# A decoder trunk on one core: sixteen tiles of the first FFN by seven block products, with sums of weights made by DMA

## The chip, the cores and the metric

The kernel runs on one core of a Trainium2 chip. The core has TensorE (matmuls, with a separate path for loading the stationary operand), VectorE, ScalarE and GpSimd for element-wise work, and DMA queues issued from SyncE (SP), ScalarE and GpSimd. In the profile they are PE (PEld for its weight loads), DVE, ACT, POOL and SP. The metric is the device time of one execution in microseconds; a kernel is given by the median of its runs.

## The reference

The reference is a trunk of two layers on a residual stream x of 512 tokens by 1024 channels, in float32. Layer 0 is a Conformer convolution module, layer 1 a RetNet retention; each is followed by a ConvFFN, and a last RMSNorm ends it. Each block reads `rmsnorm(x, g)`, that is x times rstd (one number per token) times a gain per channel, and is added to x. The change is in the FFN of layer 0:

```python
def conv_ffn(x, w_in, dw_w, dw_b, w_out):
    h = x @ w_in                              # (512, 1024) @ (1024, 2 * 2816)
    a, u = jnp.split(h, 2, axis=-1)
    a = causal_dwconv(a, dw_w, dw_b)          # width 3 over the tokens
    return (jax.nn.silu(a) * u) @ w_out       # (512, 2816) @ (2816, 1024)
```

## The kernel before

**Layout.** The residual lies in SBUF transposed: eight tiles `xT[k]` of 128 channels by 512 tokens. The 2816 inner channels of an FFN are 22 inner tiles of 128 channels. A result tile of the first matmul is 128 inner channels by 512 tokens, one PSUM bank; there are eight banks.

**Three products for one.** Every float32 operand is split into a high part, rounded to TensorE's fast float32 format (`fp32r`), and a low part, the rest; a product is three matmuls, high by high, low by high and high by low (`mm3`, lines 271 to 274). ScalarE makes the high part of weights (line 229), VectorE the low part (line 233), in pieces of 128 x 1024; four buffers of each part are there (`wh`, `wl`), and four for raw weights (`wr`), which SP loads from DRAM (line 202). The function `weights()` (line 265) hands out the next unit of weights and emits the loading and splitting of the unit after it. Units are used in the order in which `_chunks()` (line 75) lists them.

**The FFN.** `HALVES` (line 29) cuts the 22 inner tiles into groups of 12 and 10. For each group `ffn_half` (line 785) makes, per inner tile, eight `mm3` for a and eight for u on the split x times gain, 48 matmuls of 512 columns. The factor rstd is applied afterwards, as it is only known by then: `evac` (line 804) multiplies a by the broadcast rstd `norm.rb` (line 812, VectorE), applies the three taps (line 814 on ScalarE, lines 815 and 816 on VectorE) and Silu (line 817), multiplies by rstd once more for u (line 818, GpSimd), then by u (line 820, VectorE), and splits the result y. `evac` of a tile is emitted after the matmuls of the next one. `proj_out` (line 398) then multiplies the y of a group by `w_out` and adds to `xT` (line 430, VectorE); with a `norm` given, it also begins the next normalisation. Its weights come in chunks of up to four inner tiles.

**What else runs there.** The rotary tables of layer 1 (`rotary_tables`, line 836) are a generator of GpSimd steps; in the first FFN one step is issued per inner tile, tied behind that tile's scaling and product by `issue_after` (line 823).

**Seven products in layer 1.** `ret_vg_blocks` (line 1013) makes the v and gate of a retention head by a Strassen-Winograd scheme on two-by-two blocks: seven block products in place of eight. The sums on the side of x are made once, by `left_sums` (line 916) from x times gain times rstd (`normed`, line 911); sums of weights are made on VectorE in SBUF (line 255). Its matmuls have 512 columns.

**Order.** Each engine has one queue that it works off in order. A planner lays out the instructions from the traced program; `issue_after` and `pe_in_order` tie an instruction behind another one of the same engine.

## Time and profile before

| | before |
|---|---|
| median of 3 runs | 1293.9 us (1293.53 to 1294.2) |
| the profiled execution | 1293.24 us, span 1291.5 us |
| first FFN in the trace | 182.3 to 543.5 us |
| TensorE, VectorE, ScalarE, GpSimd busy | 1282.0, 810.0, 520.9, 355.2 us |
| TensorE's granted clock | 0.999 |
| moved by DMA | 140.48 MB, mean 109 GB/s |

The span runs from the first to the last instruction of the profiled execution; some 1.7 us of its time lie around it. A row of instruction groups gives line, engine, operation, output and inputs, shape, count, then busy time, mean duration in ns, and idle time before it with what ended that. A row of the windows gives, per engine, busy time and the number of instructions. A matmul's duration includes its way through the array, so matmuls overlap, and their pace is the distance between two starts.

### The profile page before, as it was taken

What the parts mean: (1) busy time and instruction counts of PE and PEld (TensorE: products, weight loads), DVE (VectorE), ACT (ScalarE), POOL (GpSimd) and SP (SyncE); (2) the same over time, 40 slices, a digit from 0 to 9 for tenths busy, and PEclk for the clock granted to TensorE, in tenths of its full rate; (3) what the DMA queues carried; (4) which work ended last, traced back from release to release, by engine and by line L of the source; (5) the groups of instructions that cost most, each with busy time, mean ns of one, the idle gap of its engine ahead of it and who ended that gap; (6) DMA issues with size and microseconds to landing.
All of it is one profiled execution on the core that took longest, in us unless ns stands there. A gap on an engine that the chain in (4) does not pass through costs nothing.

```text
span 1291.5 us, 15110 instructions
## 1 busy us (share of the span) xinstructions
PE 1282.0 (99%) x5955; PEld 1067.0 (83%) x5955; DVE 810.0 (63%) x1036; ACT 520.9 (40%) x703; POOL 355.2 (28%) x305
## 2 busy tenths in 40 slices
PE   9999999999999999999999999999999999999997
PEld 7889988888888888888888888878888888888886
DVE  6998657665335554579696596596675643355542
ACT  6646644333124333334435335354443431233332
POOL 0957323797006110221311312304211110011111
PEclk9999999999999999999999999999999999999999
DMA  9533422313221313323314405323224342213111
GB/s 330 225 123 106 148 98 70 127 66 130 98 98 66 130 49 114 131 81 106 106 42 160 138 14 180 103 83 116 97 76 145 94 143 98 98 66 131 33 65 65
DMA packets 35926, 140.48 MB, mean 109 GB/s; under 512 B 10896, under 2 KB 15760, under 8 KB 21776
## 3 DMA queue, kind: packets, MB, share of 16 engines
q1 hardware_dynamic: 32256, 134.02, 30.2%
q10 hardware_dynamic: 3600, 5.52, 1.5%
q8 instruction: 46, 0.75, 0.2%
q14 instruction: 24, 0.20, 0.0%
HBM read 130.08 MB, written 2.10 MB: 102 GB/s over the span
## 4 chain that ended last, share of the span: by engine, by line
PE 96%; DVE 2%; issue 1%; ACT 0%; POOL 0%; POOLq 0%
PE fa L272 6%; PE fa L274 6%; PE fu L273 6%; PE fu L272 6%; PE fu L274 6%; PE fa L273 6%; PE lo L272 3%; PE fo L273 3%; PE fo L274 3%; PE lo L273 3%; PE lo L274 3%; PE fo L272 3%; PE cph L539 2%; PE ro L272 2%; PE ro L273 2%; PE ro L274 2%
## 5 line engine op out<-in xcount | busy, mean ns | idle before, releaser
L233 DVE TENSOR_TENSOR wl<-wr,wh 128x1024 fp32r<-128x1024 f32 (+2 forms) x242 | 302.7, 1254 | 207.2 <-ACT wh L229 203.7
L229 ACT CAST wh<-wr 128x1024 fp32r<-128x1024 f32 (+2 forms) x244 | 250.5, 1029 | 372.0 <-PE fo L274 82.7
L811 POOL MEMSET ap<- 128x2 f32 x44 | 4.2, 99 | 371.7 <-DVE ft L816 305.4
L988 POOL TENSOR_TENSOR gg<-gg,gn 128x512 f32<-128x512 f32 x16 | 27.5, 1719 | 179.3 <-ACT gg L987 179.3
L820 DVE TENSOR_TENSOR fy<-fu,ft 128x512 f32<-128x512 f32 x44 | 30.4, 690 | 68.6 <-PE fu L274 35.0
L814 ACT ACTIVATE ft<-ap,prm 128x512 f32<-128x512 f32 x44 | 35.8, 814 | 71.3 <-DVE ap L812 71.3
L588 DVE SCALAR_TENSOR_TENSOR tp<-hp,prm,tp 128x512 f32<-128x512 f32 x80 | 55.8, 747 | 0.4
L579 POOL TENSOR_TENSOR pla<-pla,plt 128x512 f32<-128x512 f32 x36 | 49.1, 1365 | 9.8 <-ACT pla L575 5.7
L815 DVE SCALAR_TENSOR_TENSOR ft<-ap,prm,ft 128x512 f32<-128x512 f32 x44 | 37.2, 844 | 17.7 <-ACT ft L814 17.5
L817 ACT ACTIVATE ft<-ft 128x512 f32<-128x512 f32 x44 | 27.9, 633 | 45.0 <-DVE ft L816 44.6
L972 POOL TENSOR_TENSOR rs<-rs 128x512 f32<-128x512 f32 x16 | 24.7, 1559 | 67.5 <-DVE rs L971 43.7
L818 POOL TENSOR_TENSOR ft<-ft,n3r 128x512 f32<-128x512 f32 x22 | 32.1, 1461 | 29.0 <-ACT ft L817 29.0
L818 POOL TENSOR_TENSOR ft<-ft,n1r 128x512 f32<-128x512 f32 x22 | 31.6, 1434 | 28.8 <-ACT ft L817 28.8
L816 DVE SCALAR_TENSOR_TENSOR ft<-ap,prm,ft 128x512 f32<-128x512 f32 x44 | 35.8, 814 | 1.5
L578 ACT ACTIVATE plt<-hp,prm 128x512 f32<-128x512 f32 x36 | 25.8, 722 | 20.6 <-POOL pla L579 20.2
L539 PEld LDWEIGHTS cph<-ph,cmat 128*128 128x128 f32 x288 | 32.6, 192 | 0.2
L539 PE MATMUL cph<-ph,cmat 128*128 128x128 f32 x288 | 32.6, 275 | 0.0
L430 DVE TENSOR_TENSOR xT<-ro,xT 128x512 f32<-128x512 f32 x32 | 21.6, 682 | 15.6 <-PE ro L274 15.6
L255 DVE TENSOR_TENSOR wr<-wr,wr 128x1024 f32<-128x1024 f32 x24 | 28.8, 1211 | 0.0
L812 DVE TENSOR_TENSOR ap<-fa,n3r 128x512 f32<-128x512 f32 x22 | 15.1, 690 | 20.5 <-PE fa L274 20.5
L812 DVE TENSOR_TENSOR ap<-fa,n1r 128x512 f32<-128x512 f32 x22 | 15.1, 689 | 17.2 <-PE fa L274 17.2
L856 POOL TENSOR_SCALAR near<-prod 128x512 f32<-128x512 f32 x11 | 22.9, 2085 | 0.9
(1851 smaller groups left out, 3842.1 us busy)
## 6 DMA issues: line engine op xcount, KB each, us to landing
wr<-in_weights_dram SPq DMA_DIRECT2D x106, 1024.0 KB, 4.9
cmat<-in_mats_dram SPq DMA_DIRECT2D x4, 2304.0 KB, 10.6
wr<-in_weights_dram SPq DMA_DIRECT2D x4, 512.0 KB, 3.4
wr<-in_weights_dram SPq DMA_DIRECT2D x6, 256.0 KB, 6.8
yt<-yq ACTq DMA_DIRECT2D x24, 64.0 KB, 2.1
yt<-yq SPq DMA_DIRECT2D x24, 64.0 KB, 2.1
xt<-xq SPq DMA_DIRECT2D x32, 48.0 KB, 2.0
xT<-in_xt_dram SPq DMA_DIRECT2D x4, 256.0 KB, 4.4
```

Source lines behind the costliest of these rows:

```text
L229: latest[0] = act.copy(hi[:, o:o + n], raw[:, s + o:s + o + n])
L233: latest[1] = low_on.get(i, dve).tensor_tensor(out=lo[:, o:o + n], in0=raw[:, s + o:s + o + n], in1=hi[:, o:o + n].bitcast(F32), op=ALU.su ...
L272: pe.matmul(ps, wh, xh, start=first, stop=False, **check)
L273: pe.matmul(ps, wl, xh, start=False, stop=False, **check)
L274: pe.matmul(ps, wh, xl, start=False, stop=last, **check)
L539: pe.matmul(ps[:, g * P:(g + 1) * P], mats[i][g][:, s, :], ph[:, g, NSH - 1 - s:NSH - 1 - s + P], start=s == 0, stop=s == NSH - 1)
L579: gate[0] = pool.tensor_tensor(out=pl, in0=pl, in1=tm, op=ALU.add).ins
L588: dve.scalar_tensor_tensor(out=a, in0=hp[:, t:t + S], scalar=tap(t, i), in1=a, op0=ALU.mult, op1=ALU.add)
L814: act.activation(t, ap[:, 2:], AF.Identity, scale=wc(2), bias=wc(3))
L815: dve.scalar_tensor_tensor(out=t, in0=ap[:, 1:1 + S], scalar=wc(1), in1=t, op0=ALU.mult, op1=ALU.add)
L816: dve.scalar_tensor_tensor(out=t, in0=ap[:, 0:S], scalar=wc(0), in1=t, op0=ALU.mult, op1=ALU.add)
L818: scaled = pool.tensor_tensor(out=t, in0=t, in1=norm.rb, op=ALU.mult)
```

## The change

- The first FFN has four groups of inner tiles, 6, 6, 6 and 4 (`GROUPS[0]`). The first stays as it was, the other sixteen tiles go by `ffn_blocks`. The second FFN keeps 12 and 10.
- `ffn_blocks` takes two inner tiles at a time: four weight blocks (two halves of the 1024 input channels, times the a and u parts, 256 columns each) against four blocks of x (two halves of the channels, two halves of the tokens). Seven products each go over 2 tiles x 4 blocks of 128 channels x 3 matmuls of 256 columns (256 tokens). They accumulate into banks z, x and p, six of the eight; between products ScalarE copies z out (`kept`, q1, u1, u2), and VectorE forms the four results from banks and copies.
- x is taken times gain and rstd (`Factors`), so that these tiles need no rstd afterwards: the pass of line 818 and that of line 812 fall away for them. The sums on the side of x (`sums_of`) are made on VectorE and ScalarE during the first group, and all eight x tiles are multiplied and split anew (`normed_split`) into the slots of the old ones behind it.
- The four sums of weights, a, b, c and d, are made in DRAM per group (`make_sums`): eight DMAs issued from GpSimd, in the order of its instructions, four of them copies and four adding to what is there. Each is 128 x 1024 float32 per pair of tiles, for a whole group at once. Those of the second group are issued during the first, those of each later group during the one before. The loads of the products then take single blocks or sums of 512 KB, seven to a pair.
- The rotary steps all go beside the first group, two to a tile, without the tie behind the tile's own work.

```diff
-HALVES = [(0, 12), (12, 22)]
+GROUPS = [[(0, 6, False), (6, 12, True), (12, 18, True), (18, 22, True)], [(0, 12, False), (12, 22, False)]]
...
-        for f0, f1 in HALVES:
-            for f in range(f0, f1, 2):
+        for f0, f1, by_blocks in GROUPS[l]:
+            if by_blocks:
+                pairs.append((len(out), (f1 - f0) // 2))
+                for kc, part in ((0, 0), (0, 1), (1, 0), (1, 1)):
+                    for f in range(f0, f1, 2):
+                        cols("ffn_w_in", l, 512 * kc, 4, (F * part + f * P, 256))
+            for f in range(f0, f1, 2) if not by_blocks else ():
...
+    def pool_in_order():
+        return tc.issue_after(next(i for i in reversed(nc.cur_bb.bb.instructions) if i.engine == mybir.EngineType.Pool))
...
+        n = dict(pairs).get(i)
+        if n:
+            units += [(i, (j, which)) for j in range(n) for which in (0, 2, "a", "b", "c", "d", 3)]
+            i += 4 * n
+            continue
...
+        if isinstance(n, tuple):
+            j, which = n
+            raw = wp.tile([P, 2048], F32, tag="wr", bufs=4, name=f"wr{i}_{j}{which}")
+            src = block(i, which)[:, j] if isinstance(which, int) else made[i][which][:, j]
+            nc.sync.dma_start(raw[:, :1024], src)
+            for _ in split_raw(raw, i, unit):
+                pass
+            return
...
+    def make_sums(i):
+        made[i] = {which: dp.tile([P, dict(pairs)[i], 1024], F32, tag="sum", bufs=8, name=f"sum{i}{which}")
+                   for which in "abcd"}
+        a, b, c, d = (made[i][which] for which in "abcd")
+        def copy(dst, src):
+            with pool_in_order():
+                pool.dma_start(dst, src)
+        def add(dst, src):
+            with pool_in_order():
+                pool.dma_start(dst, src, accum_op=ALU.add)
+        copy(a, block(i, 0))
+        copy(c, block(i, 1))
+        yield
+        add(a, block(i, 1))
+        add(c, block(i, 3))
+        yield
+        copy(b, a)
+        yield
+        add(b, block(i, 3))
+        yield
+        copy(d, b)
+        yield
+        add(d, block(i, 2))
...
+    class Factors:
+        def __init__(self, norm, xs, pool_, other):
+            self.norm, self.xs, self.other = norm, xs, other
+            self.sums = [pool_.tile([P, 4, 4, N2], F32R, tag=f"s{half}", bufs=1, name=f"{norm.name}s{half}") for half in "hl"]
+        def normed(self, k):
+            n = self.norm
+            t = xp.tile([P, S], F32, tag="nsq", bufs=2, name=f"{n.name}n{k}")
+            dve.scalar_tensor_tensor(out=t, in0=xT[k], scalar=n.gain[:, k:k + 1], in1=n.rb, op0=ALU.mult, op1=ALU.mult)
+            return t
+        def sums_of(self, k):
+            x1, x2 = self.normed(k), self.normed(k + 4)
+            lo, hi = slice(0, N2), slice(N2, S)
+            a = xp.tile([P, 2, N2], F32, tag="nacc", bufs=1, name=f"{self.norm.name}sa{k}")
+            b = self.other(f"{self.norm.name}sb{k}")
+            dve.tensor_tensor(out=a[:, 0], in0=x1[:, hi], in1=x2[:, hi], op=ALU.subtract)
+            dve.tensor_tensor(out=a[:, 1], in0=a[:, 0], in1=x1[:, lo], op=ALU.subtract)
+            dve.tensor_tensor(out=b[:, 0], in0=x1[:, lo], in1=x1[:, hi], op=ALU.subtract)
+            dve.tensor_tensor(out=b[:, 1], in0=x2[:, lo], in1=a[:, 1], op=ALU.add)
+            for o, t in ((0, a), (2, b)):
+                h, l = (u[:, k, o:o + 2, :] for u in self.sums)
+                act.copy(h, t)
+                dve.tensor_tensor(out=l, in0=t, in1=h.bitcast(F32), op=ALU.subtract)
+        def normed_split(self, k):
+            self.xs[k] = split(self.normed(k), f"{self.norm.name}n{k}", ("xh", "xl"), xp8)
...
+    def ffn_blocks(fp, l, norm, f0, f1, left, side=None):
+        ys = []
+        for f in range(f0, f1, 2):
+            def bank(which):
+                return [psum(f"f{which}{l}_{f + j}")[:, :N2] for j in range(2)]
+            def product(pss, which, first=False):
+                w = weights()
+                for j, ps in enumerate(pss):
+                    for k, (xh, xl) in enumerate(left.factor(which)):
+                        mm3(ps, *w(k, j * P, (j + 1) * P), xh, xl, first and k == 0, k == 3, skip_group_check=not first)
+            def kept(pss, name):
+                tiles = [fp.tile([P, N2], F32, tag=name, bufs=2, name=f"{name}{l}_{f + j}") for j in range(2)]
+                for t, ps in zip(tiles, pss):
+                    act.copy(t, ps)
+                return tiles
+            lo, hi = slice(0, N2), slice(N2, S)
+            aps = [fp.tile([P, S + 32], F32, tag="ap", bufs=2, name=f"ap{l}_{f + j}") for j in range(2)]
+            us = [fp.tile([P, S], F32, tag="fy", bufs=2, name=f"fy{l}_{f + j}") for j in range(2)]
+            z = bank("z")
+            product(z, "x11", True)
+            q1 = kept(z, "q1")
+            x = bank("x")
+            product(x, "x12", True)
+            for j in range(2):
+                dve.memset(aps[j][:, :2], 0.0)
+                dve.tensor_tensor(out=aps[j][:, 2:2 + N2], in0=x[j], in1=q1[j], op=ALU.add)
+            p = bank("p")
+            product(p, "s1", True)
+            product(z, "s2")
+            u1 = kept(z, "u1")
+            product(z, "s3")
+            u2 = kept(z, "u2")
+            for j in range(2):
+                dve.tensor_tensor(out=us[j][:, hi], in0=p[j], in1=u2[j], op=ALU.subtract)
+            product(z, "x22")
+            ts = []
+            for j in range(2):
+                act.copy(aps[j][:, 2 + N2:2 + S], z[j])
+                ts.append(taps(fp, l, f + j, aps[j]))
+            product(p, "s4")
+            for j in range(2):
+                dve.tensor_tensor(out=us[j][:, lo], in0=p[j], in1=u1[j], op=ALU.subtract)
+                dve.tensor_tensor(out=us[j], in0=us[j], in1=ts[j], op=ALU.mult)
+                ys.append(split(us[j], f"y{l}_{f + j}", ("yh", "yl"), fp))
+            if side is not None:
+                next(side, None)
+                next(side, None)
+        return ys
...
+            t = taps(fp, l, f, ap)
...
+            if each is not None:
+                next(each, None)
...
-        fp = es.enter_context(tc.tile_pool(name="f0", reuse_waits="tile", bufs=12))
+        fp = es.enter_context(tc.tile_pool(name="f0", reuse_waits="tile", bufs=6))
         rp = es.enter_context(tc.tile_pool(name="rot", reuse_waits="tile", bufs=1))
-        n2 = Norm(mix_g[1], "n2")
+        groups = GROUPS[0]
+        making = [make_sums(i) for i, _ in pairs[:len(groups) - 1]]
         rot = rotary_tables(rp)
-        for n, (f0, f1) in enumerate(HALVES):
-            ys = ffn_half(fp, 0, n1, f0, f1, () if n else (None, n1.stats, n1.bcast), rot)
-            proj_out(ys, f"fo{n}", n2 if n else None)
+        left = Factors(n1, list(n1.xs), fp, lambda name: fp.tile([P, 2, N2], F32, tag="fy", bufs=2, name=name))
+        def each():
+            for f in range(groups[0][1] - 1):
+                next(making[0], None)
+                next(rot, None)
+                next(rot, None)
+                if f:
+                    left.sums_of(f - 1)
+                yield
+        next(making[0])
+        ys = ffn_half(fp, 0, n1, *groups[0][:2], (None, n1.stats, n1.bcast), each=each())
         for _ in rot:
             pass
+        for k in range(KD):
+            left.normed_split(k)
+        for _ in making[0]:
+            pass
+        proj_out(ys, "fo0", None)
+        for n, (f0, f1, _) in enumerate(groups[1:], 1):
+            side = making[n] if n < len(making) else None
+            ys = ffn_blocks(fp, 0, n1, f0, f1, left, side)
+            for _ in side or ():
+                pass
+            n2 = Norm(mix_g[1], "n2") if n == len(groups) - 1 else None
+            proj_out(ys, f"fo{n}", n2)
...
```

More of the change, by code (lines that the diff above doesn't have):

```diff
@@ L75, in _chunks @@
 def _chunks():
-    out, blocks = [], []
+    out, blocks, pairs = [], [], []
     def cols(w, l, r0, nk, *ranges):
@@ L128, in _chunks @@
     ffn(1)
-    return out, blocks
+    return out, blocks, pairs
 LINE = 256
@@ L258, in emit_weights, with block @@
             pass
+    made = {}
+    def block(i, which):
+        n = dict(pairs)[i]
+        return weights_d[i + which * n:i + (which + 1) * n, :, :1024].rearrange("c p n -> p c n")
+    def make_sums(i):
[21 more added lines that the diff above has]
+        add(d, block(i, 2))
     def weights_ahead(n):
@@ L782, in trunk, with factor @@
         proj_out(zs, "co", n1, between=lambda k: run(SEQ_OUT.get(k, "")))
-    def ffn_half(fp, l, norm, f0, f1, hooks=(), side=None):
+    N2 = S // 2
+    class Factors:
[22 more added lines that the diff above has]
+            self.xs[k] = split(self.normed(k), f"{self.norm.name}n{k}", ("xh", "xl"), xp8)
+        def factor(self, which):
+            if which[0] == "s":
+                j = int(which[1]) - 1
+                return [tuple(u[:, k, j, :] for u in self.sums) for k in range(4)]
+            t = slice(0, N2) if which[1] == "1" else slice(N2, S)
+            return [tuple(u[:, t] for u in self.xs[k + (4 if which[2] == "2" else 0)]) for k in range(4)]
@@ new lines, in taps, with wc @@
+    def taps(fp, l, f, ap):
+        def wc(j):
+            return fw[l][:, j * NF + f:j * NF + f + 1]
+        t = fp.tile([P, S], F32, tag="ft", bufs=3, name=f"ft{l}_{f}")
+        act.activation(t, ap[:, 2:2 + S], AF.Identity, scale=wc(2), bias=wc(3))
+        dve.scalar_tensor_tensor(out=t, in0=ap[:, 1:1 + S], scalar=wc(1), in1=t, op0=ALU.mult, op1=ALU.add)
+        dve.scalar_tensor_tensor(out=t, in0=ap[:, 0:S], scalar=wc(0), in1=t, op0=ALU.mult, op1=ALU.add)
+        act.activation(t, t, AF.Silu)
+        return t
@@ L786, in ffn_half @@
+    def ffn_half(fp, l, norm, f0, f1, hooks=(), side=None, each=None):
         ys, wt, mid = [], {}, {}
@@ L904, in trunk @@
         hooks = [n2.stats, n2.bcast, fold]
-        sums = [rt.tile([P, 4, 4, N2], F32R, tag=f"s{half}", bufs=1, name=f"s{half}") for half in "hl"]
-        def normed(k):
-            t = xp.tile([P, S], F32, tag="nsq", bufs=2, name=f"xn{k}")
-            dve.scalar_tensor_tensor(out=t, in0=xT[k], scalar=n2.gain[:, k:k + 1], in1=n2.rb, op0=ALU.mult, op1=ALU.mult)
-            return t
-        def left_sums(k):
-            x1, x2 = normed(k), normed(k + 4)
-            lo, hi = slice(0, N2), slice(N2, S)
-            a = xp.tile([P, 2, N2], F32, tag="nacc", bufs=1, name=f"sa{k}")
-            b = rt.tile([P, 2, N2], F32, tag="u2", bufs=1, name=f"sb{k}")
-            dve.tensor_tensor(out=a[:, 0], in0=x1[:, hi], in1=x2[:, hi], op=ALU.subtract)
-            dve.tensor_tensor(out=a[:, 1], in0=a[:, 0], in1=x1[:, lo], op=ALU.subtract)
-            dve.tensor_tensor(out=b[:, 0], in0=x1[:, lo], in1=x1[:, hi], op=ALU.subtract)
-            dve.tensor_tensor(out=b[:, 1], in0=x2[:, lo], in1=a[:, 1], op=ALU.add)
-            for o, t in ((0, a), (2, b)):
-                h, l = (u[:, k, o:o + 2, :] for u in sums)
-                act.copy(h, t)
-                dve.tensor_tensor(out=l, in0=t, in1=h.bitcast(F32), op=ALU.subtract)
-        def normed_split(k):
-            xs[k] = split(normed(k), f"xn{k}", ("xh", "xl"), xp8)
-        def left(which):
-            if which[0] == "s":
-                j = int(which[1]) - 1
-                return [tuple(u[:, k, j, :] for u in sums) for k in range(4)]
-            t = slice(0, N2) if which[1] == "1" else slice(N2, S)
-            return [tuple(u[:, t] for u in xs[k + (4 if which[2] == "2" else 0)]) for k in range(4)]
+        left = Factors(n2, xs, rt, lambda name: rt.tile([P, 2, N2], F32, tag="u2", bufs=1, name=name))
         def ret_qk(h, yt=None):
@@ L1023, in product @@
                 for tb in range(2):
-                    for k, (xh, xl) in enumerate(left(which)):
+                    for k, (xh, xl) in enumerate(left.factor(which)):
                         t = slice(tb * P, (tb + 1) * P)
```

25 lines of the change are left out of this document (9 added, 16 removed).

## The prediction

> **What bounds the kernel now.** I read the page first, then the waits of TensorE, then busy time by stretch.
>
> ```profile
> span 1291.5 us, 15110 instructions
> ...
> PE 1282.0 (99%) x5955; PEld 1067.0 (83%) x5955; DVE 810.0 (63%) x1036; ACT 520.9 (40%) x703; POOL 355.2 (28%) x305
> ```
>
> ```profile
> PE warm L171 <- POOL ones L287: 1.0, 1, 1.0
> PE vg3z L274 <- DVE wl L233: 0.5, 1, 0.5
> PE vg3p L274 <- DVE wl L233: 0.5, 1, 0.5
> PE qk L274 <- DVE n2x6l L352: 0.2, 1, 0.2
> ```
>
> ```profile
> core 0: us, PE busy (x) PEld busy (x) DVE busy (x) ACT busy (x) POOL busy (x), PEclk, DMA share, GB/s
> 182.30:543.50 361.20, 361.20 (x1595) 298.70 (x1594) 191.75 (x208) 125.33 (x152) 123.29 (x99) 1.00 0.28 96
> ```
>
> ```profile
> 649.00:741.00 92.00, 92.00 (x414) 76.59 (x413) 68.11 (x88) 39.80 (x52) 20.06 (x13) 1.00 0.35 111
> ```
>
> TensorE sets the time: all its waits come to 2.2 us. The first FFN is the stretch from 182.3 to 543.5 us, and in it TensorE never stops, at full clock. Fewer or shorter matmuls there shorten the run one for one, provided that the other engines keep up: VectorE is at 191.75 of 361.2 us (53%). The second window is one retention head, which already works by seven products: VectorE is at 74% there, and TensorE does not wait.
>
> **The matmuls.** Sixteen tiles now take 16 x 2 x 8 x 3 = 768 matmuls of 512 columns. Afterwards 8 pairs take 7 products x 2 tiles x 4 blocks x 3 = 1344 matmuls of 256 columns. The trace has both widths, accumulating into one bank:
>
> ```profile
> 205.47 0.39 PE L272 MATMUL fa<-n1x0h,wh 128*128 128x512 f32 x1
> ...
> 210.91 0.39 PE L272 MATMUL fu<-n1x0h,wh 128*128 128x512 f32 x1
> ```
>
> ```profile
> 666.83 0.28 PE L272 MATMUL sc<-qk100h,qk110h 128*128 128x256 f32 x1
> ...
> 668.15 0.28 PE L274 MATMUL sc<-qk101l,qk111h 128*128 128x256 f32 x1
> ```
>
> 24 steps of 512 columns take 5.44 us, 226.7 ns each; 11 steps of 256 columns take 1.32 us, 120.0 ns each, 6.7 ns more than half. So 768 x 0.2267 = 174.1 us become 1344 x 0.1200 = 161.3 us: **-12.8 us**, not the eighth (21.8 us) that the count of multiplications alone would give. The output projections keep their number of matmuls.
>
> The Trainium skill (TensorE: Matmul & The Clock Gate, Back-to-back issue gap) gives a spacing of N/2.4 + 2.5 ns at full clock, by which 512 and 256 columns would cost 215.8 and 109.2 ns and the edit would save 19.0 us. Both rows above are some 11 ns longer, so the trace does not agree, and the measured spacing is used.
>
> **VectorE.** What is added has these prices:
>
> ```profile
> L233 DVE TENSOR_TENSOR wl<-wr,wh 128x1024 fp32r<-128x1024 f32 x232 | 297.0, 1283 | 205.2 <-ACT wh L229 201.7 <-PE vg3z L273 0.3
> ...
> L815 DVE SCALAR_TENSOR_TENSOR ft<-ap,prm,ft 128x512 f32<-128x512 f32 x44 | 37.2, 844 | 17.7 <-ACT ft L814 17.5
> L816 DVE SCALAR_TENSOR_TENSOR ft<-ap,prm,ft 128x512 f32<-128x512 f32 x44 | 35.8, 814 | 1.5
> L820 DVE TENSOR_TENSOR fy<-fu,ft 128x512 f32<-128x512 f32 x44 | 30.4, 690 | 68.6 <-PE fu L274 35.0 <-POOL ft L818 33.6
> ...
> L913 DVE SCALAR_TENSOR_TENSOR xn<-xT,prm,n2r 128x512 f32<-128x512 f32 x16 | 13.3, 850 | 0.1
> ...
> L430 DVE TENSOR_TENSOR xT<-fo,xT 128x512 f32<-128x512 f32 x16 | 10.8, 685 | 8.9 <-PE fo L274 8.9
> ...
> L925 DVE TENSOR_TENSOR sb<-xn,sa 128x256 f32<-128x256 f32 x4 | 1.7, 423 | 0.1
> ```
>
> A pair by products needs seven weight splits (7 x 1.28) and per tile three half-width sums (3 x 0.42), the two taps (0.84 + 0.81), the product and the low part (0.69 each): 9.0 + 2 x 4.3 = 17.6 us, against 168 x 0.12 = 20.2 us of matmuls, 87%. Over the whole FFN it gains 24 splits (30.8), 16 residual additions (10.9, four projections instead of two), the sums of x (4 x (2 x 0.85 + 4 x 0.42 + 2 x 0.69) = 19.0), the eight normed splits (8 x 1.54 = 12.3) and some 0.5 us a tile (8): 191.75 + 81 = 273 of 348 us, 78%. That is near the head's 74%, where TensorE did not wait, so I put the mean load at nothing and price the three tight places.
>
> **Place one: from plain tiles to products.** In the 65 us of the six plain tiles, VectorE gets 11.1 us a tile (two splits 2.6, evacuation 3.8, sums 4.75) against 48 x 0.2267 = 10.9 us. The normed splits reuse the slots of x, so they cannot start before the last plain matmuls. Behind the last evacuation (3.8) and 12.3 us of these stands the split of the second weight chunk of the projection, 1.3 us: ready 17 us after the matmuls, wanted after one chunk, 4 x 12 matmuls, 10.9 us. GpSimd is also fuller: two rotary steps a tile, which no longer are tied behind the tile's own product.
>
> ```profile
> 250.09 1.51 POOL L863 TENSOR_SCALAR prod<-rc 128x512 f32<-128x512 f32 x1
> ...
> 255.24 1.29 POOL L871 TENSOR_TENSOR turn<-turn,prod 128x512 f32<-128x512 f32 x1
> ```
>
> One step spans 6.4 us, two and the scaling some 14.3 us in 10.9, so the scaling of tiles 4 and 5, wanted at the same second chunk, may come late too. Both waits end at one place, so the later counts, not the sum. Bounds: 0 (the queues are ordered well, as at the same step of the retention, where the list of waits shows none) to 12 us. I take **+4**, nearer the first.
>
> **Place two: a bank copied and at once used again.** The second product into z is copied by ScalarE (u1) and the next product accumulates into the same bank; the same with u2 and x22. The second bank is finished at the end of the product and wanted again 12 x 0.12 = 1.44 us later.
>
> ```profile
> 695.64 1.03 ACT L229 CAST wh<-wr 128x1024 fp32r<-128x1024 f32 x1
> 696.57 0.58 ACT L1030 COPY uu<-vg1z 128x512 f32<-128x512 f32 x1
> ```
>
> ```profile
> L1078 ACT CAST sch<-sct 128x256 fp32r<-128x256 f32 x4 | 1.6, 410 | 2.2 <-DVE sct L1075 2.2
> ```
>
> In the head such a copy stood behind a weight cast, hidden since half a product lasts 2.72 us there. Here a cast just begun and one or two copies take 1.03 + 0.41 to 0.82 = 1.4 to 1.9 us: a wait of 0 to 0.5 us at 16 places, 0 to 8 us. Most copies will find ScalarE free, so I take 0.15 us each, **+2.4**.
>
> **Place three: the last group has four tiles.** Its projection has two earlier tiles to start with, 6 x 0.2267 = 1.4 us, while the last pair still needs half-width sum, product, cast and low part (0.42 + 0.69 + 0.62 + 0.69 = 2.4 us, the second tile about 4). 0 to 3 us; I take **+1**, since TensorE can begin other output tiles.
>
> ```profile
> L348 ACT CAST y_9h<-fy 128x512 fp32r<-128x512 f32 x2 | 1.3, 626 | 1.8 <-DVE fy L820 1.8
> ```
>
> **The sums in DRAM.** No row shows a DRAM to DRAM copy or an adding DMA. The nearest are the weight loads:
>
> ```profile
> wr<-in_weights_dram SPq DMA_DIRECT2D x106, 1024.0 KB, 4.9
> ```
>
> ```profile
> GB/s 0 0 0 0 0 0 0 0 0 51 267 0 0 0 0 0 56 131 384 449 178 0 84 122 440 431 131 0 0 84 253 412 440 9 0 0 150 337 440 272
> ```
>
> At 440 GB/s 1.05 MB take 2.4 us of the 4.9, so 2.5 us are fixed. A block for three pairs is 1.57 MB: 6.1 us alone, 9.6 for two together. The chain is two copies, two adds, copy, add, copy, add; if an add costs a copy, 2 x 9.6 + 4 x 6.1 = 44 us. Loads take more than before as well: 7 x 0.52 MB in 20.2 us is 182 GB/s, 41% of that peak, and some 22% in the projections; about a third on average, which stretches the chain to 65 us. It is released from the end of the first pair of the group before (20 us) and its last sum is wanted in the sixth product of the next group, 20.2 x 3 + 32.6 + 14.4 = 107 us: 87 us are there. The first chain has about as much (adds issued after the first evacuation, some 25 us in). So it is hidden, and I take 0. An add of twice a copy gives 58 us, stretched 87: just enough. Cover gone, SP's queue stands at the load of the sum, and every later weight load behind it. On GpSimd the adds wait for the copies with the rotary steps and the scaling of the plain tiles behind them; in the product groups nothing stands behind.
>
> **Sum.** -12.8 + 4 + 2.4 + 1 = -5.4 us. The profiled execution took 1293.24 us (span 1291.5 and 1.7 around it), 0.66 under the median of 1293.9: 1287.8 by it, **1288.5 us** as a median.
>
> **Rivals.** (a) **All three places are hidden**: 1293.9 - 12.8 = 1281.1 us. For it: the head at 74% without waits. Against: products last 2.9 us here, 5.4 there.
>
> (b) **VectorE becomes the bound**: splits queue behind evacuations that wait for a product, and each pair costs at least the 96 x 0.2267 = 21.8 us that it costs now. The saving is gone (1293.9) and place one remains: 1294 to 1300, about 1296. For it: 87% in an in-order queue. Against: four buffers of split weights.
>
> (c) **The adds are slow**, and TensorE waits for sums at the beginning of the product groups. It decides from an add of more than two copies. At three (2 x 9.6 for the copies becomes 9.6 + 24, and so on: 72 us, stretched 108) the third group starts 21 us late; at four (87, stretched 130) it is 43 late, the other two some 12 together. +21 to +55, with the places: 1310 to 1343, about 1320. For it: nothing in the trace has this operation. Against: only that even two copies fit.
>
> The Trainium skill (Collectives: The Full Stack, The bandwidth ceiling: the fold count and why AG ≠ RS ≠ AR) says a reduction in the DMA path reads two sources and runs at about half the rate of a copy. No run here shows it yet; by it the chain would be the 87 us just worked out, at the edge of the cover, and (c) would begin with any further slowing.
>
> **How the numbers follow.** The forecast (1284 to 1291) has 0.38, (a) 0.20, (b) 0.23, (c) 0.19. A change of 0.2%, 2.6 us, is about what can be told apart: faster is below 1291.3, slower above 1296.5. Faster: all of (a), nearly all of the forecast and none of the others, 0.55. (b) is split, 0.12 on each side of 1296.5: same 0.15 with the forecast's upper edge, slower 0.30 with (c). The range reaches from (a), 1280, over (b) to the first part of (c), 1312, and leaves out most of (c); the likeliest case's own range is 1284 to 1291.
>
> **What would show it.** 1344 matmuls of 256 columns at 120 ns; waits of TensorE on ScalarE's copies of z, a few tenths each; one wait of some us at the second chunk of the first projection; none on SP's loads of sums. Wrong would be: a matmul spacing above 126 ns, VectorE's splits at the head of TensorE's waits in every pair, or a stop of ten us or more at the third or fourth product of a group, which is (c).

## The result and the profile after

The changed kernel takes 1328.13 us (median of 4, 1324.87 to 1329.42) against 1293.84 (1293.53 to 1294.2): a ratio of 1.0261, 95% interval 1.024 to 1.0282. It is 34 us slower, and the predicted 1288.5 us and the range up to 1312 are missed. The profiled execution took 1324.87 us.

The page of the changed kernel, its first lines and the granted clock in 40 slices:

```profile
span 1323.1 us, 16622 instructions
...
PE 1282.7 (97%) x6531; PEld 1091.1 (82%) x6531; DVE 896.3 (68%) x1172; ACT 571.0 (43%) x807; POOL 358.6 (27%) x297
...
PEclk9999999799999999989999999999999999999999
```

TensorE now idles for 40 us of the span (before, 9.5), and its clock dips in two slices of the first FFN. The windows cut this FFN into three stages, used for every kernel below. **A** runs from the first plain matmul (182.3 us) to the first product's; **B** from there into the last product into z (in the change, 0.8 us before its last matmul starts); **C** from there to the broadcast of the next norm's rstd. The changed kernel:

```profile
182.30:309.80 127.50, 106.20 (x440) 83.97 (x439) 105.57 (x115) 44.33 (x60) 94.81 (x65) 0.93 0.61 163
309.80:542.60 232.80, 227.86 (x1611) 214.99 (x1610) 145.09 (x201) 116.80 (x174) 17.37 (x18) 0.99 0.81 248
542.60:586.10 43.50, 38.96 (x174) 31.38 (x173) 31.25 (x37) 19.75 (x29) 10.90 (x7) 0.92 0.31 107
```

And the kernel before over the same work:

```profile
182.30:554.90 372.60, 372.28 (x1643) 307.32 (x1642) 199.92 (x217) 129.23 (x157) 127.43 (x101) 1.00 0.29 98
```

What the three stages would take without a wait follows from the matmuls. A: 6 tiles x 48 x 0.2267 = 65.3, a projection of 6 tiles 32.6, and 1.3 for the norm's own small matmuls: 99.2 (the runs below without a wait there have 98.9 to 99.4). B: 8 pairs x 168 x 0.120 = 161.3, two projections 65.3, less the product behind the last z (2.9): 223.7. C: 2.9, a projection of 4 tiles 21.8 and 11.0 to the broadcast (as e7 below has it, so e7's own loss in C is nothing by this choice): 35.7. Together 358.6, 14.0 below the 372.6 of before; 12.8 of them are the matmuls of the predicted sum, the rest lies behind the last projection. The trace has 403.8: A is 28.3 us over, B 9.1, C 7.8, in sum 45.2. Idle TensorE is 30.7 of it (21.3, 4.9 and 4.5: length less PE busy); of the other 14.5, some 8 us were added to matmuls in four stretches, 27.3 us together, in which the granted clock was 0.50. The rest is waits too short to leave TensorE idle: a matmul's record of 0.39 us covers more than the 0.227 to the next start.

The waits of TensorE in the first FFN and just behind it (us in all, times, longest):

```profile
PE fa L333 <- ACT wh L247: 9.1, 1, 9.1
PE fo L334 <- DVE wl L251: 5.2, 3, 2.8
PE fz L333 <- ACT u L907: 4.0, 2, 3.2
PE fa L334 <- DVE wl L251: 2.4, 1, 2.4
PE fo L335 <- DVE y_5l L410: 2.1, 1, 2.1
PE qk L335 <- DVE n2x7l L413: 1.9, 1, 1.9
PE qk L335 <- DVE n2x6l L413: 1.4, 1, 1.4
```

**Stage A.** The longest wait, 9.1 us, is on a weight cast in the middle of the plain tiles. GpSimd's timeline shows where it begins:

```profile
214.10 1.25 POOL L305 DMA_DIRECT2D sum22a<-in_weights_dram  x1
227.34 1.13 POOL L305 DMA_DIRECT2D sum22c<-in_weights_dram  x1 [11.99 <-issue]
...
229.85 0.63 POOL L978 MEMSET ap<- 128x2 f32 x1
```

GpSimd issues the first add, and then for 11.99 us does nothing that the profile shows ("issue"); the second add begins at 227.34. The memset and scaling of the next plain tile stand behind it, and VectorE's product (L983) behind them. ScalarE's queue stands at the cast of this product's result, and the weight casts that TensorE waits for are behind that cast. Meanwhile the clock of TensorE falls to half:

```profile
DVE fy L983 <- POOL ap L978: 12.8, 1, 12.8
```

```profile
232.46 0.62 ACT L409 CAST y_1h<-fy 128x512 fp32r<-128x512 f32 x1 [12.87 <-DVE fy L983]
...
236.84 1.99 ACT L247 CAST wh<-wr 128x1024 fp32r<-128x1024 f32 x2
```

```profile
222.00:232.00 10.00, 6.79 (x30) 5.29 (x29) 0.26 (x1) 0.00 (x0) 4.66 (x6) 0.97 0.60 101
232.00:242.00 10.00, 1.69 (x3) 1.09 (x4) 10.00 (x12) 3.45 (x5) 7.58 (x6) 0.50 1.03 275
```

From 232 us VectorE is full, and what it missed is not caught up before the projection, where TensorE waits for its low parts and for the last y (the rows of fo).

**Stage B.** Products come 120 ns apart, as predicted:

```profile
449.74 0.28 PE L334 MATMUL fp<-n1sh,wl 128*128 128x256 f32 x1
...
450.82 0.28 PE L334 MATMUL fp<-n1sh,wl 128*128 128x256 f32 x1
```

Nine steps take 1.08 us. The DMA share of this stage is 0.81, and the loads beside the sums are late. Issues from 300 to 480 us (count, KB, median us to landing):

```profile
wr<-in_weights_dram SPq DMA_DIRECT2D x22, 512.0 KB, 8.0
...
sum38b<-sum38a POOLq DMA_DIRECT2D x1, 1536.0 KB, 17.6
sum38b<-in_weights_dram POOLq DMA_DIRECT2D x1, 1536.0 KB, 18.0
```

The same row of e1 below, without sums, has 3.8. With fewer loads beside them, at 257 to 277 us, a copy and an add of 1.5 MB took:

```profile
sum22d<-sum22b POOLq DMA_DIRECT2D x1, 1536.0 KB, 6.7
sum22d<-in_weights_dram POOLq DMA_DIRECT2D x1, 1536.0 KB, 11.6
```

**Stage C.** The next layer's first product waits for the last four splits of its norm (the rows of qk); before, that wait was 0.2 us.

### The profile page after: what moved, and what is told of

Same layout as the page of the kernel before. It is cut to its first block, busy times and chain, and to the rows that moved or that the text cites. A ratio compares the mean times of both kernels' runs of the same rounds, so it can differ in the third digit from the quotient of the medians.

```text
span 1323.1 us, 16622 instructions
## 1 busy us (share of the span) xinstructions
PE 1282.7 (97%) x6531; PEld 1091.1 (82%) x6531; DVE 896.3 (68%) x1172; ACT 571.0 (43%) x807; POOL 358.6 (27%) x297
## 4 chain that ended last, share of the span: by engine, by line
PE 84%; DVE 9%; issue 3%; POOL 2%; DMA 2%; ACT 1%; POOLq 0%; ACTq 0%; DVEq 0%
PE fu L333 3%; PE fa L333 3%; PE fu L334 3%; PE fa L334 3%; PE fu L335 3%; PE fa L335 3%; PE lo L333 3%; PE lo L334 3%; PE lo L335 3%; PE cph L600 2%; PE fo L335 2%; PE fo L333 2%; PE fo L334 2%; DVE wl L251 2%; PE qk L335 2%
## 5 line engine op out<-in xcount | busy, mean ns | idle before, releaser
L251 DVE TENSOR_TENSOR wl<-wr,wh 128x1024 fp32r<-128x1024 f32 (+2 forms) x234 | 294.9, 1264 | 173.2 <-ACT wh L247 171.3
L247 ACT CAST wh<-wr 128x1024 fp32r<-128x1024 f32 (+2 forms) x236 | 241.7, 1027 | 298.0 <-PE lo L334 70.8
L983 DVE TENSOR_TENSOR fy<-fu,ft 128x512 f32<-128x512 f32 x28 | 19.3, 688 | 47.7 <-PE fu L335 21.0
L333 PE MATMUL fz<-n1sh,wh 128*128 128x256 f32 x128 | 37.0, 290 | 4.0 <-ACT u L907 4.0
L441 POOL TENSOR_TENSOR n2acc<-n2acc,n2sq 128x512 f32<-128x512 f32 x6 | 9.9, 1643 | 106.7 <-ACT n2sq L440 106.3
L334 PE MATMUL fp<-n1sh,wl 128*128 128x256 f32 x128 | 36.3, 285 | 0.9 <-DVE wl L251 0.8
L952 DVE SCALAR_TENSOR_TENSOR ft<-ap,prm,ft 128x512 f32<-128x512 f32 x44 | 36.4, 828 | 1.0
L334 PE MATMUL fz<-n1sh,wl 128*128 128x256 f32 x128 | 37.0, 289 | 0.1
L335 PE MATMUL fz<-n1sl,wh 128*128 128x256 f32 x128 | 36.9, 289 | 0.0
L335 PE MATMUL fp<-n1sl,wh 128*128 128x256 f32 x128 | 36.1, 283 | 0.0
L333 PE MATMUL fp<-n1sh,wh 128*128 128x256 f32 x128 | 35.8, 284 | 0.0
L639 ACT ACTIVATE plt<-hp,prm 128x512 f32<-128x512 f32 x36 | 25.8, 722 | 20.7 <-POOL pla L640 20.2
L600 PEld LDWEIGHTS cph<-ph,cmat 128*128 128x128 f32 x288 | 32.6, 192 | 0.2
```

The costliest lines, as they stand in the source:

```text
L247: latest[0] = act.copy(hi[:, o:o + n], raw[:, s + o:s + o + n])
L251: latest[1] = low_on.get(i, dve).tensor_tensor(out=lo[:, o:o + n], in0=raw[:, s + o:s + o + n], in1=hi[:, o:o + n].bitcast(F32), op=ALU.su ...
L333: pe.matmul(ps, wh, xh, start=first, stop=False, **check)
L334: pe.matmul(ps, wl, xh, start=False, stop=False, **check)
L335: pe.matmul(ps, wh, xl, start=False, stop=last, **check)
L600: pe.matmul(ps[:, g * P:(g + 1) * P], mats[i][g][:, s, :], ph[:, g, NSH - 1 - s:NSH - 1 - s + P], start=s == 0, stop=s == NSH - 1)
```

## Experiments

Two theories stood against each other after this reading. By the first, the adding DMAs lose the time, through their issue and their traffic. By the second, VectorE and GpSimd are overloaded by the other work that the change put beside the plain tiles. The table has the time of the profiled execution and, for each stage, the us over its matmuls; for groups of 6, 4, 6, 6 these are 99.2, 212.8 and 46.6 (the four-tile projection falls into B, the last has six). Executions of one kernel that makes the sums differ by up to 4.8 us, so single differences below that aren't read; the kernel before had 1293.2 to 1293.6 beside all of them.

| kernel | groups | us | A over | B over | C over |
|---|---|---|---|---|---|
| the change | 6,6,6,4 | 1324.87 | 28.3 | 9.1 | 7.8 |
| e1_plain | 6,6,6,4 | 1304.62 | 16.7 | 1.1 | 7.2 |
| e2_one_add | 6,6,6,4 | 1337.03 | 22.1 | 28.4 | 6.8 |
| e3_rot_late | 6,6,6,4 | 1337.18 | 12.4 | 37.6 | 7.4 |
| e4_last6 | 6,4,6,6 | 1342.6 | 25.5 | 37.4 | 0.0 |
| e5_ring2 | 6,6,6,4 | 1321.31 | 20.3 | 1.2 | 6.3 |
| e9_ring2_aligned | 6,6,6,4 | 1312.67 | 18.8 | 7.1 | 7.0 |
| e6_plain_rotlate | 6,6,6,4 | 1291.07 | 0.1 | 4.7 | 6.8 |
| e7_plain_rotlate_last6 | 6,4,6,6 | 1282.12 | -0.3 | 2.9 | 0.0 |
| e8_early | 6,4,6,6 | 1325.89 | 1.0 | 18.7 | 0.1 |
| e10_all | 6,4,6,6 | 1307.93 | 0.2 | 28.0 | 0.0 |
| e11_all_ahead | 6,4,6,6 | 1308.66 | 0.6 | 28.3 | 0.0 |
| e12_gpsimd_sums | 6,4,6,6 | 1322.91 | 0.0 | 43.0 | 0.1 |

**e1_plain: no sums are made.** The products load plain blocks in their place, with the same loads and matmuls, so this kernel's output is not the reference's; the same holds for e6 and e7.

```diff
-            src = block(i, which)[:, j] if isinstance(which, int) else made[i][which][:, j]
+            src = block(i, which if isinstance(which, int) else "abcd".index(which))[:, j]
-        making = [make_sums(i) for i, _ in pairs[:len(groups) - 1]]
+        making = [iter([None]) for _ in pairs[:len(groups) - 1]]
```

> The eight copying and adding DMAs per group are left out; the products that took sums a, b, c, d load the four plain weight blocks instead, so the output is not the reference's, and all other work is the same. The changed kernel loses 28.3 us between the first plain matmul and the first product (309.8 - 182.3 = 127.5 us against 99.2 of matmuls), 8.1 us in the product groups and 8.3 us at the hand-over to the retention. Theory A (the issue of the adding DMAs holds GpSimd's queue, and behind it VectorE and TensorE; in the product groups their traffic delays the loads): of the 28.3 us some 14 go (the 9.1 and 2.4 us waits and the lower clock after them), of the 8.1 some 6, the hand-over stays: 1306 to 1310. Theory B (VectorE's own work in the first group is the bound, the hold only falls together with it): at most 5 us go in all: 1322 to 1327.

1304.62 us: the sums cost some 20 us, as the first theory says. But 16.7 of stage A's loss stay, and nearly all of C's: these have another cause, which e6 and e7 show.

**e2_one_add: one add to a step**, so that the second add is issued later.

```diff
         add(a, block(i, 1))
+        yield
         add(c, block(i, 3))
```

> One edit: the second of the two adds that stand side by side is issued one step later, so each step issues a single add. The bytes and the work are the same. In the changed kernel GpSimd stands 12 to 15.7 us in the issue of each second add. Theory A: this stand goes, TensorE's 9.1 us wait on a weight cast goes with it, and the time falls by 8 to 14 us, to 1314 to 1320. Theory B: the stand moves or goes and the time stays within 4 us of 1328.

1337.03 us, against both. GpSimd's timeline shows the second add still held, and the waits of SP's queue show what moving it did:

```profile
214.04 1.25 POOL L305 DMA_DIRECT2D sum22a<-in_weights_dram  x1
227.83 1.22 POOL L305 DMA_DIRECT2D sum22c<-in_weights_dram  x1 [8.82 <-issue]
```

```profile
SPq L265 <- DMA sum22d<-in_weights_dram: 20.7, 1, 20.7
```

It is issued 13.8 us behind the first (13.2 in the change), although a step lies between. The last sum of the first chain came a step later, and every weight load stood behind it for 20.7 us: the chain has no slack.

**e3_rot_late: the rotary steps** go behind the pairs of the product groups.

```diff
-                next(rot, None)
-                next(rot, None)
                 if f:
                     left.sums_of(f - 1)
...
+            with pool_in_order():     # at the end of each pair
+                next(rot, None)
+                next(rot, None)
```

> The rotary steps leave the first group: two steps behind each pair of the product groups, the rest before the last projection. VectorE was busy from 232 to 302 us without a gap in the changed kernel while GpSimd ran rotary steps beside it. Theory B (VectorE's work bounds the first group, and GpSimd's rotary steps lengthen it: two-input operations of 1.1 us last 1.5 to 1.8 us beside them): 8 to 15 us go, 1313 to 1320. Theory A: only the hold counts, GpSimd's rotary steps are not on the path, at most 4 us go: 1324 to 1329.

1337.18 us, above both. A falls by 16 us as the second theory says, but B loses 28 more. There GpSimd's queue alternates rotary steps with adds that wait for copies; the sums come late and the weights behind them:

```profile
PE fx L334 <- DVE wl L251: 15.9, 1, 15.9
PE fz L333 <- ACT u L907: 11.6, 3, 8.8
```

**e4_last6: the last group has six tiles.**

```diff
-GROUPS = [[(0, 6, False), (6, 12, True), (12, 18, True), (18, 22, True)], ...
+GROUPS = [[(0, 6, False), (6, 10, True), (10, 16, True), (16, 22, True)], ...
```

> The groups are 6, 4, 6, 6 in place of 6, 6, 6, 4; nothing else. Theory: the hand-over to the retention costs 8.3 us because the last projection is short (four tiles, 21.8 us), all eight output tiles end in its last 8 us, and eight additions, eight splits and five weight splits stand on VectorE at once; with six tiles the first four output tiles end 16 us before the others, and 4 to 8 us go: 1320 to 1324. Rival: the hand-over is set by the norm's own chain, whatever the length, and the time stays within 3 us of 1328.

1342.6 us, above both. But the loss in C is gone, so the short last group is its cause. The group of four, though, covers less of the next chain, and SP waits for its sums:

```profile
SPq L265 <- DMA sum32b<-in_weights_dram: 26.0, 1, 26.0
SPq L265 <- DMA sum32d<-in_weights_dram: 18.6, 1, 18.6
```

**e5_ring2 and e9_ring2_aligned: twice the memory for the descriptors of GpSimd's DMAs.** In e5 a pad of 192 bytes was dropped and a small constant moved to make room; e9 keeps the place of all larger tiles modulo 256 bytes (there the room comes from a smaller pad and from two tiles of a few bytes with two buffers instead of four).

```diff
-    nc = _bacc.Bacc("TRN2", target_bir_lowering=False, num_devices=1, dynamic_dma_scratch_size=1024)
+    nc = _bacc.Bacc("TRN2", target_bir_lowering=False, num_devices=1, dynamic_dma_scratch_size=2048)
-    by_phase = cp.tile([P, PH, WIDE // PH], F32, name="by_phase")
+    by_phase = cv.tile([P, PH, WIDE // PH], F32, tag="by_phase", bufs=1, name="by_phase")
-    sp.tile([P, 3 * LINE // 16], F32, tag="pad", bufs=1, name="pad")
+    sp.tile([P, 16], F32, tag="pad", bufs=1, name="pad")     # e9; no pad in e5
```

> Edit: the memory that holds the descriptors of GpSimd's DMAs is twice as large; nothing else of the order changes (a small constant lies in another pool to make room). Theory 1 (the 12.0 us for which GpSimd stands in the issue of the second add are a lack of room for its descriptors until the first add has drained): the stand shrinks below 3 us, VectorE no longer waits for the plain tile's first step, stage one (first plain matmul to first product, 127.5 us in the changed kernel) falls by 8 to 12 us, 1316 to 1321 us in all. Theory 2 (an adding DMA's issue itself costs that long, or waits for the one before it whatever room there is): stand and time stay, 1325 to 1331.

> Edit: as the run with twice the descriptor memory, but every tile keeps its place in SBUF modulo 256 bytes. In that run the moving operands lay 64 bytes further (modulo 256), and matmuls of 512 columns in the second FFN came 232.0 ns apart (431 in 100 us) instead of 225.7 (443 in 100 us), which cost 14 us behind the first FFN alone. Theory 1 (the place in SBUF sets that pace): pace back at 225.7 ns, 1302 to 1308 us, so that nearly the whole price of the sums (23.5 us) was the stand in the issue and what it delayed. Theory 2 (the pace fell for another reason, the larger descriptor memory for one): 1318 to 1323 us as before.

GpSimd no longer stands still. Its timeline in e9:

```profile
214.35 1.24 POOL L305 DMA_DIRECT2D sum22a<-in_weights_dram  x1
215.06 1.71 POOL L305 DMA_DIRECT2D sum22c<-in_weights_dram  x1
...
217.71 1.07 POOL L978 MEMSET ap<- 128x2 f32 x1
```

So it was room: with 1024 bytes the second add was held until the first had landed (at 227.0 us), with 2048 it was not. The other four standstills of this kind in the change, 10.9 to 15.7 us each beside the product groups, are gone in e9 too; one was at a first add and one at a copy. Stage A falls by 8 to 9.5 us. e5 was slowed elsewhere: from the norm's broadcast to the end it took 750.8 us, against 737.0 in the changed kernel. The windows of 1070 to 1170 us in the second FFN, e5 and then e9:

```profile
1070.00:1170.00 100.00, 100.00 (x431) 80.50 (x430) 39.87 (x43) 25.93 (x28) 5.04 (x6) 1.00 0.30 103
```

```profile
1070.00:1170.00 100.00, 100.00 (x443) 82.81 (x442) 39.78 (x44) 26.63 (x29) 4.91 (x6) 1.00 0.31 106
```

431 matmuls against 443 at the same clock, 232.0 ns against 225.7. In e5 the x and y tiles, the moving operands of these matmuls, start at 160 modulo 256 bytes and in e9 at 96 as in the change, while the split weights start at 96 in both; most other tiles moved with x and y. With the places kept, the pace is back and e9 takes 1312.67 us, 12.2 below the change's profiled execution. It was expected at 1302 to 1308: 8.0 us remain against e1, where no sums are made.

**e6_plain_rotlate and e7_plain_rotlate_last6: what is left without the sums.** e6 is e1 with the edit of e3; e7 has the groups of e4 as well.

> Edit: no sums are made by DMA (the products load plain blocks, so the output is another one, with the same loads and matmuls), and the rotary steps go behind the pairs of product groups instead of beside the plain tiles. Without the sums alone the run took 1304.6 us with stage one at 115.9 us against 99.2 us of matmuls. Theory 1 (what is left of stage one's loss is GpSimd's two rotary steps per plain tile, ahead of the scaling in its queue and beside VectorE's operations): stage one 99 to 104 us, 1289 to 1294 in all. Theory 2 (it is VectorE's own added work: sums of x, normed splits): stage one stays at 112 to 116 us, 1301 to 1305.

> Edit: as the run without sums and with the rotary steps late, and the groups are 6, 4, 6 and 6 instead of 6, 6, 6 and 4. If the loss at the hand-over to the next norm (6.7 us without the sums) comes from the short last group, this takes 5 to 7 us off: 1283 to 1288 us, about what the prediction had for all places hidden (1281.1), and the causes named add up to the whole. If the loss lies in the hand-over itself whatever the group's length, no change against the run with late rotary steps.

e6 came as expected with the rotary steps as the cause, and e7 0.9 us below the span given for the short last group. Stage A is at its matmuls once the rotary steps are gone from it. The groups of VectorE from 200 to 280 us, e1 and then e6:

```profile
L861 DVE SCALAR_TENSOR_TENSOR n1n<-xT,prm,n1r 128x512 f32<-128x512 f32 x15 | 17.0, 1161 | 0.0
L251 DVE TENSOR_TENSOR wl<-wr,wh 128x1024 fp32r<-128x1024 f32 x11 | 17.0, 1547 | 0.0
...
L983 DVE TENSOR_TENSOR fy<-fu,ft 128x512 f32<-128x512 f32 x6 | 4.1, 677 | 0.0
```

```profile
L251 DVE TENSOR_TENSOR wl<-wr,wh 128x1024 fp32r<-128x1024 f32 x15 | 18.2, 1215 | 6.9 <-ACT wh L247 6.9
L861 DVE SCALAR_TENSOR_TENSOR n1n<-xT,prm,n1r 128x512 f32<-128x512 f32 x16 | 12.3, 806 | 0.0
```

The same operation took 1161 ns beside the rotary steps and 806 without, a low part 1547 and 1215. The product that reads one operand from PSUM (L983 in e1) took 677 and 680: it wasn't lengthened. Nor was every operation with two inputs in SBUF: the second tap (L952 in e1) took 741 and 915. The windows from 230 to 280 us of the two have VectorE (third pair of numbers) at 49.71 and at 43.00 of 50 us, with GpSimd (fifth) at 37.86 and 23.62. So in e1 it is VectorE's own time that is full, and not a wait of VectorE for GpSimd's queue:

```profile
230.00:280.00 50.00, 42.26 (x167) 32.79 (x166) 49.71 (x59) 20.82 (x29) 37.86 (x22) 0.93 0.16 53
```

```profile
230.00:280.00 50.00, 50.00 (x223) 41.40 (x222) 43.00 (x60) 21.11 (x29) 23.62 (x15) 1.00 0.26 87
```

The Trainium skill (SBUF — State Buffer, Summary: rules for kernel authors) says that where a VectorE operation has two inputs in SBUF while GpSimd reads SBUF, the second to issue waits until the first ends; the lengthening of these two-input operations agrees. In e7 TensorE has two waits left:

```profile
PE fz L333 <- ACT u L907: 1.4, 1, 1.4
PE qk L335 <- DVE n2x6l L413: 0.3, 1, 0.3
```

So the steps lead from the change's profiled 1324.9 us down: descriptor room -12.2 (e9), the rest of the sums -8.0 (e1), rotary steps -13.6 (e6), short last group -9.0 (e7), to 1282.1, which is 11.3 below before. Each step is the difference of two kernels, so that they add up says nothing by itself; the first two carry the scatter of single executions. And they hold in this order only: 1282.1 with the 8.0 of the sums put back would be 1290.1, and e10 below, which has the sums and the other three causes taken away, takes 1307.9.

**e8_early: sums one group earlier**, the first chain between the convolution's GpSimd operations; with the edits of e2 to e5.

```diff
-SEQ = ("m0 m1 m2 b3 b4 t0 m3 t1 m4 t2 m5 p3 ...
+SEQ = ("m0 m1 m2 b3 b4 t0 k m3 t1 m4 t2 k m5 p3 ...      # k: next(making[0], None)
-        next(making[0])
+        next(making[1])
-            side = making[n] if n < len(making) else None
+            side = making[n + 1] if n + 1 < len(making) else None
```

> Edit: the full computation. The sums are made one group ahead of the shipped kernel's place (those of the second group in the convolution's stage, those of the third during the plain group, those of the fourth during the second), one add to a step; rotary steps behind the pairs; groups 6, 4, 6, 6; twice the descriptor memory. Theory 1 (the price of the sums was their lateness and GpSimd's stand): near the run without sums, 1285 to 1295 us, no wait of SP on a sum. Theory 2 (the price is the traffic beside the weight loads): still about 20 us above the run without sums, 1303 to 1310.

1325.89 us. It has e5's slower pace (14 us behind the FFN), and the convolution's stage ends 12 us later: GpSimd stood 8.0 us until an add had landed and 5.0 us at the next of these DMAs, each time ahead of a step of that stage's norm. Stage A is 1.0 over, B 18.7. It doesn't tell the theories apart.

**e10_all and e11_all_ahead: the full computation with all three causes taken away.** Both have e9's memory, groups 6, 4, 6, 6, and the rotary steps behind the last chain; e11 makes the sums from the third group on one group earlier.

```diff
             for _ in side or ():
                 pass
+            if n == 2:                # e11: n == 1
+                with pool_in_order():
+                    next(rot)
+                for _ in rot:
+                    pass
...
-        for _ in making[0]:           # from here on e11 only
-            pass
+        for m in making[:2]:
+            for _ in m:
+                pass
...
-            side = making[n] if n < len(making) else None
+            side = making[n + 1] if n + 1 < len(making) else None
```

> Edit: the full computation with the three causes taken away at once: twice the descriptor memory with all places kept, groups 6, 4, 6, 6, and the rotary steps behind the last sums instead of beside the plain tiles. If the three causes (stand in the issue, rotary steps beside the plain group, short last group) are the whole and the sums of the third group come in time (a chain of 84 us from the start of the second group, against 73 us of that group and its projection and some 9 to 14 us until the sums are wanted): 1283 to 1291 us. If the sums come late, as in the two runs that moved work between them, TensorE waits for them at the head of the third group: 1295 to 1310 us.

> Edit: as the run before it, but with each chain of sums made one group earlier from the third group on (the third group's behind the second group's without a pause, the fourth group's during the second), the rotary steps behind them. If lateness of the sums is what remains, this is the fastest with the full computation: 1282 to 1288 us. If their traffic beside the weight loads of the first group's projection and of the second group is, slower than the run before it, 1290 to 1300 us.

e10 takes 1310.93 us (4 runs; ratio to before 1.0133, 1.0118 to 1.0148), e11 1310.76 (1.0139, 1.0122 to 1.0156). e11 is outside both of its expected spans, and e10, though near its upper one, hasn't the waits for sums that this span rested on. A and C are nearly free of loss, and the gain is lost in B, 28 us over. Earlier sums don't help, and SP waits for no sum in either run, so it isn't their lateness. In e10, 17.3 of the 28 us are idle TensorE and some 7.6 work at a granted clock of 0.50. The longest wait of TensorE in e10, and ScalarE's timeline around the longest:

```profile
PE fz L333 <- ACT u L907: 15.3, 4, 6.4
```

```profile
314.15 1.04 ACT L247 CAST wh<-wr_1d 128x1024 fp32r<-128x1024 f32 x1 [2.83 <-DMA wr_1d<-sum22d]
318.08 1.04 ACT L247 CAST wh<-wr 128x1024 fp32r<-128x1024 f32 x1 [2.88 <-DMA wr<-in_weights_dram]
319.03 0.61 ACT L409 CAST y_7h<-fy 128x512 fp32r<-128x512 f32 x1
319.55 0.64 ACT L907 COPY u<-fz 128x256 f32<-128x256 f32 x2
```

The copy of z, for which TensorE waits, stands in ScalarE's queue behind casts of weights that are not needed yet and whose loads are late. In this stage the same 512 KB loads took 8.6 us at the median, and the DMA share from 280 to 410 us was 1.00:

```profile
wr<-in_weights_dram SPq DMA_DIRECT2D x19, 512.0 KB, 8.6
```

And in e1, without sums, from 285 to 480 us:

```profile
wr<-in_weights_dram SPq DMA_DIRECT2D x22, 512.0 KB, 3.8
```

In the change, the longest stop of B (3.2 us, to 366.9 us) ends in the same way: the copy of z starts at 366.5 behind a cast whose load took 12.1 us. In e11 the copies of z cost 8.3 us, and another stop of 9.2 is put down to VectorE by the profile. Why e9 loses 7 us here and e10 28, with as many bytes and loads of 8.0 us, was not separated; e10's second group is shorter by two tiles and its chain is no shorter.

**e12_gpsimd_sums: no adding DMA; GpSimd adds in SBUF** from four loads to a pair.

```diff
+                for q in (0, 2, 1, 3):
+                    nc.sync.dma_start(quad[q], block(i, q)[:, j])
...
+            if add is not None:
+                with pool_in_order():
+                    pool.tensor_tensor(out=quad[to], in0=quad[to], in1=quad[add], op=ALU.add)
```

> Edit: the full computation without any adding DMA. Each block of a pair is loaded once (four loads of 512 KB instead of seven), and GpSimd adds in SBUF, four additions of 128 x 1024 for each pair of tiles, between the products; groups 6, 4, 6, 6; rotary steps behind the pairs. GpSimd's addition of 128 x 1024 takes about 2.4 us (a low part of that size on GpSimd did), so 9.4 us per pair of 20.2 us of matmuls. Theory 1 (traffic of copies, adds and seven loads was what kept the sums from being free): 1282 to 1289 us, faster than before. Theory 2 (GpSimd beside VectorE lengthens VectorE's two-input operations from 1.1 to 1.7 us, as in the plain group; VectorE has 17.6 us of work per pair and gets some 3 to 5 more): VectorE becomes the bound of the product groups, 1290 to 1305 us.

1325.79 us (ratio 1.0249, 1.0232 to 1.0266): neither. The additions took 2.4 to 2.8 us on average in each group of rows and share a queue with rotary steps of some 8 us; addition, cast and low part follow one another, and TensorE waits for the weights themselves in B (43.0 over). VectorE is busy for 187.0 of the 255.9 us of B, so it isn't the bound:

```profile
PE fp L340 <- ACT wh L247: 13.6, 3, 5.9
PE fz L340 <- ACT u L914: 6.9, 5, 2.2
```

It shows that this order of GpSimd's work doesn't do, not that GpSimd can't. No kernel here beats the one before with the full computation.

## Why the prediction was wrong

**The matmuls (-12.8): right.** 120 ns hold, and with every other loss away e7 is 11.3 us below before. That is close to the rival "all three places are hidden" (1281.1 us): the idea's worth was read correctly, its price was not. The spacing that the prediction quotes from the Trainium skill (TensorE: Matmul & The Clock Gate, Back-to-back issue gap) is given there for a matmul by itself; the 120.0 and 226.7 ns are of matmuls in a row with a weight load for each.

**"Place one: from plain tiles to products" (+4, bounds 0 to 12): mis-sized, +28.3.** It failed twice. It took VectorE's durations from rows of before, and counted GpSimd's rotary steps only as a queue ahead of the scaling. e1 against e6 shows that they lengthen VectorE's operations, by which a VectorE with about as much work as time (11.1 us a tile to 10.9) became the bound: 16.7 us. Of the rest, 9.5 us are the standstill in the add's issue (the change against e9), and 2.1 came with the sums in e9 against e1. The sentence that "the adds wait for the copies with the rotary steps and the scaling of the plain tiles behind them" named the queue that was held, but costed it at nothing and looked at the copies' landing only, not at the issue.

**"The sums in DRAM" (0): wrong.** The duration of an add was about within the bounds: 11.6 us against 6.7 for a copy where the fewest loads ran beside them. Over the six pairs of a copy and the add behind it in the change, the ratio is 1.0 to 2.7, with different traffic beside each. So the half rate that the prediction takes from the Trainium skill (Collectives: The Full Stack, The bandwidth ceiling: the fold count and why AG ≠ RS ≠ AR) is neither borne out nor refuted. The chains took about what was allowed for: 87 us for the first, from its first issue at 190.2 us to its last landing at 276.8. The second took 92, 5 beyond the cover, and SP waited 9.5 us for its last sum, but no stop of TensorE followed that wait. What was not priced is the issue (12.2 us by e9) and the traffic beside the weight loads (8.0 us by e9 against e1; 25.8 in the order of e10 against e7, whose rotary steps stand elsewhere). The working stretched the chain for the loads, but not the loads for the chain. And "just enough" had no slack, as e2, e3 and e4 show, each of which delayed or shortened one piece and lost 12 to 18 us in all. In its time the result lies within the rival **(c)** (1310 to 1343), by luck: its mechanism, waits for sums at the head of the groups, is that of e4 and not of the change.

**"Place two" (+2.4): right in size alone.** Without the sums the copies of z cost 1.4 us (e7) to 3.1 (e6), in the change 4.0. Its assumption that "most copies will find ScalarE free" fails when loads are late: then the same place passes the DMA's delay on to TensorE.

**"Place three: the last group has four tiles" (+1): the place was wrong.** The projection does begin in time. The loss is behind it, 7.8 us in stage C of the change (6.8 in e6, and 9.0 in all by e7 against e6): with a shorter projection the residual additions and the next norm's splits fall together, and the first product of the next layer waits for them.

**VectorE's mean load at nothing: right.** In e7 it is busy for 72% of B (155.34 of 215.7 us) without a wait of its making; rival (b) has no part in the product groups. It is the 65 us of plain tiles where VectorE was full.

## What to carry to other kernels

An operation that costs an engine no busy time can still hold its queue: price the issue of a DMA, the room for its descriptors and what stands behind it, and price the loads beside it at the new traffic, not at the old. Before adding work to a stage, add up both engines that share it at their durations under load; in this kernel a VectorE at 11.1 of 10.9 us a tile had no way to absorb GpSimd beside it. And take the causes away one at a time with the expensive part left out (e1, e6, e7): it showed what the idea was worth, while the same edits with the sums in place (e2 to e4) each looked like a loss.

## What the runs showed that was not expected

- A second adding DMA of 1.5 MB, issued right behind the first, held GpSimd for 12.0 us with 1024 bytes for descriptors and for nothing that the profile shows with 2048.
- The place of tiles in SBUF changed the pace of matmuls: in e5 the x and y tiles lay 64 bytes further modulo 256 than in e9, the split weights did not, and matmuls of 512 columns came 232.0 ns apart instead of 225.7, 14 us behind the first FFN alone. That it is x and y and not another tile that moved with them isn't shown.
- The stop of 9.1 us lasted from 228.8 to 237.9 us; from 231.5 us to some 7 us beyond its end the granted clock was 0.50.
